# Two pairs of heads in one chain of the recurrence of a decoder layer

## The chip, the cores and the metric

The kernel runs on one core of a Trainium2 chip. The metric is the time of one execution on the device, in microseconds. A core has five engines that run side by side, each with its own list of instructions in a fixed order: PE (TensorE, matrix products), ACT (ScalarE), DVE (VectorE), POOL (GpSimd) and SP (SyncE, here the queue of weight loads). PE writes into PSUM, eight banks of 128 rows by 512 f32 values; ACT and DVE read it from there into SBUF, the on-chip memory in which operands of products lie.

## The reference

The layer is: a SwiGLU feed-forward, a mixer (windowed attention beside an RWKV-7 recurrence of 16 heads of size 64, both gated), cross-attention into a fixed memory, a second feed-forward, and a norm. There are 256 tokens and a model width of 2048, all in f32. The part that the change touches is the recurrence:

```python
def step(S, inp):
    r_t, w_t, k_t, v_t, a_t, b_t = inp
    sa = jnp.einsum('bhij,bhj->bhi', S, a_t)
    S = S * w_t[:, :, None, :] + sa[..., None] * b_t[:, :, None, :] + v_t[..., None] * k_t[:, :, None, :]
    return S, jnp.einsum('bhij,bhj->bhi', S, r_t)
```

The result y of each head is then normed over its 64 values, gets a bonus term and a gate, and goes through w_proj_rwkv.

## The kernel before, in words

Nearly all of PE's time goes into the dense products: weights come from HBM in units of two 128-row blocks by 512 columns, ACT rounds each unit to a high part (line 339), DVE forms the low part (line 340), and PE multiplies high by high, low by high and high by low (lines 412 to 414), 512 columns a product. All other work of the mixer is cut into small steps by Python generators, which `Interleave` keeps in groups. `product` calls `bg.tick()` after every six wide products, and a tick takes the next step of the first generators of each group, as many as the group's limit. So the order of instructions on each engine comes from when the steps are called, and a scheduler may then move an instruction behind others of its engine while what it needs isn't free.

The recurrence is computed without a loop over tokens, in two chunks of 128 tokens. Heads are treated in pairs, two heads of size 64 making 128 rows. There are 16 heads in two halves of eight (h = 0, 1); a half has four pairs j. A generator `pair(h, j)` (lines 1162 to 1252) carries one pair through both chunks c. In each chunk it does, a step a tick:

- the masked products (lines 1178 to 1189): three kinds (keys by removal, keys by receptance, removal keys by receptance), for each of the two heads e one product of 64 rows (rows 0 to 63 or 64 to 127), 128 x 128 results. Head e's three results go to a tr bank of its own, 384 of 512 columns; DVE multiplies each bank by the masks into mk, 128 x 384;
- u and nt (lines 1193 to 1206) into one tr bank, and two copies by ACT;
- v0, v1, w and sa (`stage`, lines 1210 to 1226), each two products of 64 columns into an mm bank and a copy of 128 x 128 by ACT, each needing the one before; in the first chunk also the transposes bk of the keys (lines 1228 to 1232) in a tr bank;
- the output y (lines 1236 to 1245): products whose result has 64 rows (L1238, L1240), for both heads, and in the first chunk the state s0 for the second (lines 1242 to 1250).

The generators stand in the group chain with limit 3: up to three pairs go on at the same time, and between two ticks stand six wide products. PSUM is shared: three banks acc (dense products), three mm, two tr. Everything else that needs a tr bank (transposes at line 600, norms, values) shares those two. SBUF tiles of 128 x 1024 come from a ring t4 of N4 = 20 slots. `finish` (from line 1257) norms y of two pairs, and the projection by w_proj_rwkv starts behind it.

Of the kernel before, what the change touches and what calls it, by code (L numbers as in the profile page):

```python
# [7 lines left out]
F32 = mybir.dt.float32  # L8
F32R = mybir.dt.float32r
AF = mybir.ActivationFunctionType  # L10
ALU = mybir.AluOpType
# [4 lines left out]
P = 128  # L16
T = 256
# [12 lines left out]

UP, DOWN = 2.0**40, 2.0**-40
GROUPS = ((0, 4), (4, 4), (8, 3))
N4 = 20

AHEAD, LOADED = 2, 4

# [96 lines left out]
def decoder_layer(ctx: ExitStack, tc: tile.TileContext, a: dict, out: bass.AP):  # L133
    nc = tc.nc
    act, dve, pool, pe = nc.scalar, nc.vector, nc.gpsimd, nc.tensor
# [32 lines left out]
    def idle(n):  # L168
        for _ in range(n):
            yield  # L170
# [596 lines left out]
    with tc.tile_pool(name="mx", bufs=1, reuse_waits="tile") as sp:  # L767
# [3 lines left out]
        def t4(name, shape=(P, 4, T), dt=F32):  # L771
            return sp.tile(list(shape), dt, tag="t4", name=name, bufs=N4)

# [378 lines left out]
                    pool.dma_start(r[q, :, : 32 * i], ld[q, o, : 32 * i])  # L1152
            xb[h, c] = x, r

        def small(name):
            return sp.tile([P, P], F32, tag="sm", name=name, bufs=14)

        rows = [slice(64 * e, 64 * e + 64) for e in range(2)]
        ek = dict(skip_group_check=True)
        yq = {}  # L1160

        def pair(h, j):
            yield from wait_for("inverse")
            yield from wait_for(f"ready{h}")
            if j % 2 == 0:
                yq[h, j // 2] = sp.tile([P, 2, T], F32, tag="yq", name="yq", bufs=3)
            y = yq[h, j // 2]
            if j == 0:
                for c in range(2):
                    inverse_blocks(h, c)  # L1170
            if j < 3:
                yield from idle(3 + j)
            ah, bh, kh, rh = at_[h], bt[h], aa[h], rt[h]
            s0 = None
            for c in range(2):
                cs_ = slice(c * P, (c + 1) * P)
                mk = sp.tile([P, 2, 3, P], F32, tag="mk", name="mk", bufs=3)
                b = [tr() for _ in range(2)]
                for m, (x1, x2) in enumerate(((kh, ah), (kh, rh), (bh, rh))):
                    for e, r in enumerate(rows):  # L1180
                        pe.matmul(  # L1181
                            b[e][:, m * P : (m + 1) * P], x1[r, j, cs_], x2[r, j, cs_],
                            start=True, stop=True,
                        )
                for e in range(2):
                    dve.tensor_tensor(
                        mk[:, e].rearrange("p m t -> p (m t)"), b[e][:, : 3 * P],
                        mask3[:].rearrange("p m t -> p (m t)"), ALU.mult,
                    )
                yield  # L1190
                vp = vtok[h][:, c, j * P : (j + 1) * P]
                x, rr = xb[h, c]
                b = tr()
                for e, r in enumerate(rows):
                    pe.matmul(b[:, r], mk[:, e, 0, :], vp[:, r], start=e == 0, stop=c == 0, **ek)
                if c:
                    pe.matmul(b[:, :P], ah[:, j, cs_], s0[:], start=False, stop=True, **ek)
                for e in range(2):
                    pe.matmul(
                        b[:, (2 + e) * P : (3 + e) * P], rr[:, 4 * e + j, :], x[:, 4 * e + j, :],  # L1200
                        start=False, stop=True, **ek,
                    )
                u = small("u")
                act.copy(u[:], b[:, :P])
                nt = sp.tile([P, 2, P], F32, tag="nt", name="nt", bufs=3)
                act.copy(nt[:], b[:, 2 * P :].rearrange("p (e t) -> p e t", e=2))
                yield
                vb = mm()

                def stage(lhs, rhs, o, first, name):  # L1210
                    for e, r in enumerate(rows):
                        pe.matmul(  # L1212
                            vb[:, o : o + P][:, r], lhs(e), rhs[:, r],
                            start=first and e == 0, stop=True, **ek,
                        )
                    s = small(name)
                    act.copy(s[:], vb[:, o : o + P])
                    return s

                v0 = stage(lambda e: x[:, 4 * e + j, :], u, 0, True, "v0")  # L1220
                yield
                v1 = stage(lambda e: nt[:, e, :], v0, 0, False, "v1")
                yield
                w = stage(lambda e: nt[:, e, :], v1, P, False, "w")
                yield
                sa = stage(lambda e: nt[:, e, :], w, 0, False, "sa")
                if c == 0:
                    b = tr()
                    pe.transpose(b[:, :P], bh[:, j, cs_], ident[:])
                    pe.transpose(b[:, P : 2 * P], kh[:, j, cs_], ident[:])  # L1230
                    bk = sp.tile([P, 2, P], F32, tag="bk", name="bk", bufs=3)
                    act.copy(bk[:], b[:, : 2 * P].rearrange("p (x f) -> p x f", x=2))
                yield
                b = tr()
                if c:
                    pe.matmul(b[:, :P], s0[:], rh[:, j, cs_], start=True, stop=False, **ek)
                for e, r in enumerate(rows):
                    pe.matmul(b[r, :P], vp[:, r], mk[:, e, 1, :], start=c == 0, stop=False, **ek)  # L1238
                for e, r in enumerate(rows):
                    pe.matmul(b[r, :P], sa[:, r], mk[:, e, 2, :], start=False, stop=True, **ek)  # L1240
                if c == 0:
                    bs = b[:, P : 2 * P]
                    pe.matmul(bs, bk[:, 0, :], sa[:], start=True, stop=False, **ek)
                    pe.matmul(bs, bk[:, 1, :], vp, start=False, stop=True, **ek)
                act.copy(y[:, j % 2, cs_], b[:, :P])
                if c == 0:
                    s0 = small("s0")
                    dve.scalar_tensor_tensor(
                        s0[:], bs, dec[h][:, j : j + 1], bdup, ALU.mult, ALU.mult
                    )  # L1250
                yield
            bg.seen.add(f"y{4 * h + j}")


        yr = Act([], [], 4)
# [257 lines left out]
```

## Time and profile before

| | us |
|---|---|
| median of 3 runs (2262.24 to 2262.78) | 2262.58 |
| the profiled execution | 2263.34 |
| its span, first to last instruction | 2261.6 |
| PE busy | 2246.8 |
| DVE busy | 1778.4 |
| ACT busy | 1226.9 |
| POOL busy | 132.2 |

The span is what lies between the first and the last instruction of the profiled execution; 1.7 us of its time lie outside. Busy time of an engine counts each moment once. A matrix product's length in the trace is its way through the array, and the next one starts before it ends: how long a product holds PE is read from start to start. A product in plain f32 (those of the small steps) shows as two records; a product of lines 412 to 414, whose operands are rounded, and a transpose show as one. A form such as 64*128 gives rows and columns of the array that a product uses.

### The profile page before, as it was taken

To read this page: it belongs to the slowest core of one execution; us is meant where nothing else is said; L and a number is where in the kernel's file an instruction comes from. 1 tells how busy PE (TensorE), PEld (TensorE's weight loads), DVE (VectorE), ACT (ScalarE), POOL (GpSimd) and SP (SyncE) were. 2 spreads that over 40 slices of the span, in tenths; PEclk is the share of its full clock that TensorE was granted. 3 is DMA by queue.
4 is the path that set the end of the run, shared out by engine and by line. 5 is a ranking of instruction groups with operands and counts; after the bars stand their busy time and mean duration, and the time that the engine had idled before them with its cause. 6 is when DMAs were issued, how large, how long until landed. Compare 5 with 4: busy or idle time off the path is not lost.

```text
span 2261.6 us, 28110 instructions
## 1 busy us (share of the span) xinstructions
PE 2246.8 (99%) x10617; PEld 1845.5 (82%) x10617; DVE 1778.4 (79%) x2281; ACT 1226.9 (54%) x1653; POOL 132.2 (6%) x192
## 2 busy tenths in 40 slices
PE   9999999999999999999999999999999999999998
PEld 7888888888888877788888888888888888888886
DVE  7899989998988477886434566547899988998987
ACT  6555555555556477444435446456555455555554
POOL 1000000000001000301220030001000000000002
PEclk9999999999999999999999999999999999999999
DMA  7555565555556544666433476647555565555564
GB/s 262 186 206 199 190 210 199 186 204 205 189 200 200 161 135 155 216 214 208 147 90 100 143 257 218 203 166 271 187 203 201 191 211 198 186 205 205 186 209 145
DMA packets 219144, 432.49 MB, mean 191 GB/s; under 512 B 14108, under 2 KB 16385, under 8 KB 219009
## 3 DMA queue, kind: packets, MB, share of 16 engines
q1 hardware_dynamic: 210432, 404.78, 52.7%
q0 software_dynamic: 8112, 25.12, 3.5%
q8 instruction: 83, 1.36, 0.2%
q10 hardware_dynamic: 464, 0.79, 0.1%
q14 instruction: 53, 0.43, 0.1%
HBM read 417.56 MB, written 13.11 MB: 190 GB/s over the span
## 4 chain that ended last, share of the span: by engine, by line
PE 96%; DVE 2%; issue 1%; DMA 1%; ACT 1%; SPq 0%; POOL 0%; POOLq 0%; DVEq 0%; ACTq 0%
PE acc L412 19%; PE acc L413 19%; PE acc L414 19%; PE mm L414 8%; PE mm L412 8%; PE mm L413 8%; PE tr L600 2%; PE tr L413 2%; PE tr L412 2%; PE tr L414 2%; PE mm L1212 1%; PE tr L1181 1%; DVE lo L340 1%; DMA raw<-in_w_out_dram 0%; PE mm L827 0%
## 5 line engine op out<-in xcount | busy, mean ns | idle before, releaser
L340 DVE TENSOR_TENSOR lo<-raw,hi 128x1024 fp32r<-128x1024 f32 (+1 forms) x770 | 894.0, 1163 | 352.9 <-ACT hi L339 351.2
L339 ACT CAST hi<-raw 128x1024 fp32r<-128x1024 f32 (+1 forms) x770 | 759.7, 997 | 747.5 <-PE acc L414 528.5
L412 PE MATMUL acc<-hi,xhi 128*128 128x512 f32 (+1 forms) x1196 | 477.7, 400 | 2.1 <-ACT xhi L627 1.7
L413 PE MATMUL acc<-lo,xhi 128*128 128x512 f32 (+1 forms) x1196 | 465.7, 389 | 0.0
L414 PE MATMUL acc<-hi,xlo 128*128 128x512 f32 (+1 forms) x1196 | 465.0, 389 | 0.0
L412 PEld LDWEIGHTS acc<-hi,xhi 128*128 128x128 f32 x1196 | 225.3, 188 | 52.1 <-issue 5.5
L413 PEld LDWEIGHTS acc<-lo,xhi 128*128 128x128 f32 x1196 | 225.2, 188 | 45.8 <-issue 3.2
L414 PEld LDWEIGHTS acc<-hi,xlo 128*128 128x128 f32 x1196 | 224.6, 188 | 46.5 <-DVE xlo L628 1.0
L347 ACT CAST thi<-raw 128x1024 fp32r<-128x1024 f32 x172 | 178.9, 1050 | 57.6 <-DVE raw L368 44.2
L348 DVE TENSOR_TENSOR tlo<-raw,thi 128x1024 fp32r<-128x1024 f32 x172 | 208.3, 1220 | 0.7 <-ACT thi L347 0.4
L412 PE MATMUL mm<-hi,xhi 128*128 128x512 f32 x380 | 149.5, 393 | 0.0
L414 PE MATMUL mm<-hi,xlo 128*128 128x512 f32 x380 | 148.3, 390 | 0.0
L413 PE MATMUL mm<-lo,xhi 128*128 128x512 f32 x380 | 148.3, 390 | 0.0
L413 PE MATMUL acc<-lo,hhi 128*128 128x512 f32 x372 | 145.7, 392 | 0.8 <-DVE lo L340 0.8
L414 PE MATMUL acc<-hi,hlo 128*128 128x512 f32 x372 | 145.7, 392 | 0.0
L412 PE MATMUL acc<-hi,hhi 128*128 128x512 f32 x372 | 145.1, 390 | 0.0
L414 PEld LDWEIGHTS mm<-hi,xlo 128*128 128x128 f32 x380 | 71.4, 188 | 15.0
L413 PEld LDWEIGHTS mm<-lo,xhi 128*128 128x128 f32 x380 | 71.4, 188 | 14.4
L412 PEld LDWEIGHTS mm<-hi,xhi 128*128 128x128 f32 x380 | 71.5, 188 | 14.4
L413 PEld LDWEIGHTS acc<-lo,hhi 128*128 128x128 f32 x372 | 69.9, 188 | 15.4 <-DVE lo L340 1.2
L412 PEld LDWEIGHTS acc<-hi,hhi 128*128 128x128 f32 x372 | 69.9, 188 | 14.3
L414 PEld LDWEIGHTS acc<-hi,hlo 128*128 128x128 f32 x372 | 70.0, 188 | 13.9
(384 smaller groups left out, 3550.2 us busy)
## 6 DMA issues: line engine op xcount, KB each, us to landing
raw<-in_ffn_w_up_dram SPq DMA_DIRECT2D x88, 1024.0 KB, 5.3
raw<-in_ffn_w_down_dram SPq DMA_DIRECT2D x88, 1024.0 KB, 5.1
raw<-in_ffn_w_gate_dram SPq DMA_DIRECT2D x84, 1024.0 KB, 5.1
raw<-in_w_in_dram SPq DMA_DIRECT2D x136, 512.0 KB, 3.5
raw<-in_w_out_dram SPq DMA_DIRECT2D x32, 512.0 KB, 4.4
raw<-in_w_proj_attn_dram SPq DMA_DIRECT2D x16, 512.0 KB, 3.8
raw<-in_w_proj_rwkv_dram SPq DMA_DIRECT2D x16, 512.0 KB, 5.9
raw<-in_w_cross_kv_dram SPq DMA_DIRECT2D x16, 512.0 KB, 3.7
```

Of the source, the lines that this page charges most:

```text
L339: at["hi"] = act.copy(hi[:, s], raw[:, s])
L340: at["lo"] = dve.tensor_tensor(lo[:, s], raw[:, s], f32(hi[:, s]), ALU.subtract)
L347: act.copy(hi[:], v[:])
L348: dve.tensor_tensor(lo[:], v[:], f32(hi[:]), ALU.subtract)
L412: pe.matmul(o, xh, hi, start=first, stop=False, **how)
L413: pe.matmul(o, xh, lo, start=False, stop=False, **how)
L414: pe.matmul(o, xl, hi, start=False, stop=last, **how)
L600: pe.transpose(b[:, o : o + P], tok[:, t, col : col + P], ident[:])
L1181: pe.matmul(b[e][:, m * P : (m + 1) * P], x1[r, j, cs_], x2[r, j, cs_], start=True, stop=True,)
L1212: pe.matmul(vb[:, o : o + P][:, r], lhs(e), rhs[:, r], start=first and e == 0, stop=True, **ek,)
```

## The change

One generator now carries two pairs. `pairs(h, q)` replaces `pair(h, j)`, with j = 2q and 2q + 1; the group chain has limit 2 in place of 3.

- The masked products come from a function `masked`, in three groups of eight for both chunks together, where there were two groups of six a pair: the first two kinds of chunk 0, the third kind of both chunks, and, after sa of chunk 0, the first two kinds of chunk 1. A head's bank is filled to 512 columns, and DVE's product with the masks is 128 x 512, into a tile of the ring t4.
- u, v0, v1, w, sa hold both pairs, 128 x 256, and ACT copies both at once; nt fills a tr bank of its own for both pairs, 128 x 512, while before it shared one with u.
- The transposes bk of both pairs are made in the v0 step and in an mm bank, before in the sa step and in a tr bank.
- The outputs of both pairs stand in one tr bank, and one copy by ACT writes both.
- N4 is 22 in place of 20. The tiles of mk no longer have a ring of their own; the other rings of the chain have fewer, larger slots.
- A generator idles 4 ticks (q = 0) or 8 (q = 1) before its first step, where pairs idled 3, 4, 5 and 0.

```diff
@@ -30,7 +30,7 @@
 UP, DOWN = 2.0**40, 2.0**-40
 GROUPS = ((0, 4), (4, 4), (8, 3))
-N4 = 20
+N4 = 22
 AHEAD, LOADED = 2, 4
@@ -145,7 +145,7 @@
     bg.group("feat", 1)
     bg.group("attn", 2)
     bg.group("ew", 1)
-    bg.group("chain", 3)
+    bg.group("chain", 2)
     bg.group("norm", 1)
     bg.group("mem", 1)
@@ -1152,104 +1152,153 @@
                     pool.dma_start(r[q, :, : 32 * i], ld[q, o, : 32 * i])
             xb[h, c] = x, r
-        def small(name):
-            return sp.tile([P, P], F32, tag="sm", name=name, bufs=14)
...
         rows = [slice(64 * e, 64 * e + 64) for e in range(2)]
         ek = dict(skip_group_check=True)
         yq = {}
-        def pair(h, j):
+        def small(name, tag="sm", bufs=6):
+            return sp.tile([P, 2, P], F32, tag=tag, name=name, bufs=bufs)
+        def masked(h, js, which):
+            sides = ((aa[h], at_[h]), (aa[h], rt[h]), (bt[h], rt[h]))
+            b = [tr() for _ in range(2)]
+            for i, (m, c) in enumerate(which):
+                cs_ = slice(c * P, (c + 1) * P)
+                x1, x2 = sides[m]
+                for k, j in enumerate(js):
+                    o = (2 * i + k) * P
+                    for e, r in enumerate(rows):
+                        pe.matmul(
+                            b[e][:, o : o + P], x1[r, j, cs_], x2[r, j, cs_], start=True, stop=True
+                        )
+            t = t4("mk", (P, 2, 4, P))
+            mask = mask3[:, :2] if which[0][0] == 0 else mask3[:, 1:]
+            for e in range(2):
+                dve.tensor_tensor(
+                    t[:, e].rearrange("p (m k) t -> p m k t", m=2),
+                    b[e][:].rearrange("p (m k t) -> p m k t", m=2, k=2),
+                    mask.unsqueeze(2).to_broadcast([P, 2, 2, P]), ALU.mult,
+                )
+            return t
+        def pairs(h, q):
             yield from wait_for("inverse")
             yield from wait_for(f"ready{h}")
...
+            js = (2 * q, 2 * q + 1)
+            y = yq[h, q] = sp.tile([P, 2, T], F32, tag="yq", name="yq", bufs=3)
+            if q == 0:
                 for c in range(2):
                     inverse_blocks(h, c)
...
+            yield from idle(4 + 4 * q)
             ah, bh, kh, rh = at_[h], bt[h], aa[h], rt[h]
...
+            s0 = later = None
             for c in range(2):
                 cs_ = slice(c * P, (c + 1) * P)
...
+                if c == 0:
+                    mk = masked(h, js, ((0, 0), (1, 0)))
+                    yield
+                    later = masked(h, js, ((2, 0), (2, 1)))
+                    yield
+                vp = [vtok[h][:, c, j * P : (j + 1) * P] for j in js]
+                x, rr = xb[h, c]
+                b = tr()
+                for k, j in enumerate(js):
                     for e, r in enumerate(rows):
                         pe.matmul(
...
+                            b[:, k * P : (k + 1) * P][:, r], mk[:, e, k, :], vp[k][:, r],
+                            start=k + e == 0, stop=c == 0, **ek,
                         )
...
+                    if c:
+                        pe.matmul(
+                            b[:, k * P : (k + 1) * P], ah[:, j, cs_], s0[:, k, :], start=False,
+                            stop=True, **ek,
+                        )
+                u = small("u")
+                act.copy(u[:], b[:, : 2 * P].rearrange("p (k f) -> p k f", k=2))
                 b = tr()
...
+                for k, j in enumerate(js):
+                    for e in range(2):
+                        o = (2 * k + e) * P
+                        pe.matmul(
+                            b[:, o : o + P], rr[:, 4 * e + j, :], x[:, 4 * e + j, :],
+                            start=o == 0, stop=True, **ek,
+                        )
+                nt = sp.tile([P, 4, P], F32, tag="nt", name="nt", bufs=2)
+                act.copy(nt[:], b[:].rearrange("p (k t) -> p k t", k=4))
+                yield
+                vb = mm()
+                def stage(lhs, rhs, o, first, name):
+                    for k in range(2):
+                        for e, r in enumerate(rows):
+                            pe.matmul(
+                                vb[:, (o + k) * P : (o + k + 1) * P][:, r], lhs(k, e), rhs[:, k, r],
+                                start=first and k + e == 0, stop=True, **ek,
+                            )
+                    s = small(name)
+                    act.copy(
+                        s[:], vb[:, o * P : (o + 2) * P].rearrange("p (k f) -> p k f", k=2)
+                    )
+                    return s
+                v0 = stage(lambda k, e: x[:, 4 * e + js[k], :], u, 0, True, "v0")
+                if c == 0:
+                    b = mm()
+                    for k, j in enumerate(js):
+                        for i, z in enumerate((bh, kh)):
+                            o = (2 * k + i) * P
+                            pe.transpose(b[:, o : o + P], z[:, j, cs_], ident[:])
+                    bk = sp.tile([P, 4, P], F32, tag="bk", name="bk", bufs=2)
+                    act.copy(bk[:], b[:].rearrange("p (x f) -> p x f", x=4))
+                yield
+                v1 = stage(lambda k, e: nt[:, 2 * k + e, :], v0, 0, False, "v1")
+                yield
+                w = stage(lambda k, e: nt[:, 2 * k + e, :], v1, 2, False, "w")
+                yield
+                sa = stage(lambda k, e: nt[:, 2 * k + e, :], w, 0, False, "sa")
+                yield
+                if c == 0:
+                    mk_next = masked(h, js, ((0, 1), (1, 1)))
+                    yield
+                b = tr()
                 if c:
...
+                    for k, j in enumerate(js):
+                        pe.matmul(
+                            b[:, k * P : (k + 1) * P], s0[:, k, :], rh[:, j, cs_], start=k == 0,
+                            stop=False, **ek,
+                        )
+                for k in range(2):
+                    o = slice(k * P, (k + 1) * P)
                     for e, r in enumerate(rows):
                         pe.matmul(
...
+                            b[r, o], vp[k][:, r], mk[:, e, 2 + k, :], start=c + k == 0, stop=False,
+                            **ek,
                         )
...
+                    for e, r in enumerate(rows):
+                        pe.matmul(
+                            b[r, o], sa[:, k, r], later[:, e, 2 * c + k, :], start=False, stop=True,
+                            **ek,
+                        )
                 if c == 0:
...
+                    for k in range(2):
+                        bs = b[:, (2 + k) * P : (3 + k) * P]
+                        pe.matmul(bs, bk[:, 2 * k, :], sa[:, k, :], start=False, stop=False, **ek)
+                        pe.matmul(bs, bk[:, 2 * k + 1, :], vp[k], start=False, stop=True, **ek)
+                act.copy(y[:, :, cs_], b[:, : 2 * P].rearrange("p (k t) -> p k t", k=2))
                 if c == 0:
...
+                    s0 = small("s0", "s0", 2)
+                    for k, j in enumerate(js):
+                        dve.scalar_tensor_tensor(
+                            s0[:, k, :], b[:, (2 + k) * P : (3 + k) * P], dec[h][:, j : j + 1],
+                            bdup, ALU.mult, ALU.mult,
+                        )
+                    mk = mk_next
+                yield
+            for j in js:
+                bg.seen.add(f"y{4 * h + j}")
         yr = Act([], [], 4)
@@ -1302,8 +1351,8 @@
             bv.append(t4("bv"))
             columns4(bv[h], 16 + 4 * h, f"v{h}")
             bg.spawn("ew", values(h))
-            for j in range(4):
-                bg.spawn("chain", pair(h, j))
+            for q in range(2):
+                bg.spawn("chain", pairs(h, q))
             for i in range(2):
                 bg.spawn("norm", finish(h, i))
```

More of the change, by code (lines that the diff above doesn't have):

```diff
@@ L1190, in pair @@
-                yield
-                vp = vtok[h][:, c, j * P : (j + 1) * P]
-                x, rr = xb[h, c]
-                b = tr()
[L1194 to L1202, printed above, removed]
@@ L1211, in stage @@
+                for k in range(2):
+                    o = slice(k * P, (k + 1) * P)
                     for e, r in enumerate(rows):
                         pe.matmul(
-                            vb[:, o : o + P][:, r], lhs(e), rhs[:, r],
-                            start=first and e == 0, stop=True, **ek,
-                        )
[L1216 to L1220, printed above, removed]
@@ L1233, in pair @@
[L1233 to L1244, printed above, removed]
```

43 lines of the change are left out of this document (3 added, 40 removed).

## The prediction

> **What bounds the kernel now.** I read the page's first parts, then the waits, then the stretch in which the changed code runs, then the order of PE's instructions there, row by row.
>
> ```profile
> span 2261.6 us, 28110 instructions
> PE 2246.8 (99%) x10617; PEld 1845.5 (82%) x10617; DVE 1778.4 (79%) x2281; ACT 1226.9 (54%) x1653; POOL 132.2 (6%) x192
> PEclk9999999999999999999999999999999999999999
> PE 96%; DVE 2%; issue 1%; DMA 1%; ACT 1%; SPq 0%; POOL 0%; POOLq 0%; DVEq 0%; ACTq 0%
> ```
>
> PE is busy for 99% of the span and is 96% of the chain that ended last, at a full clock. The kernel ends when PE has issued its instructions. The changed chain runs from about 1104 us to 1285 us (L1181, its first products, starts at 1106.8). The view by windows for that stretch, and PE's own waits in it:
>
> ```profile
> core 0: us, PE busy (x) PEld busy (x) DVE busy (x) ACT busy (x) POOL busy (x), PEclk, DMA share, GB/s
> 1104.00:1285.00 181.00, 180.59 (x1185) 151.08 (x1184) 77.56 (x97) 79.08 (x177) 25.29 (x42) 1.00 0.33 99
> PE tr L1195 <- DVE mk L1186: 0.4, 2, 0.2
> ```
>
> PE idles 0.4 us of 181; DVE and ACT are busy for 43% and 44%, DMA for a third. So fewer ACT and DVE instructions buy nothing by themselves, and a gain can only come from PE's rows lying closer together. PE's number of matrix products does not change: the built order has 10,060 in both kernels. What changes is which stand next to each other, and the timeline shows that this has a price.
>
> **A masked group whose products alternate between the two heads of a pair (rows 0 to 63, rows 64 to 127), and one whose products don't.** Start, length, engine, line; each f32 product is two records. The timeline of PE:
>
> ```profile
> 1106.46 0.39 PE L414 MATMUL acc<-hi,xlo 128*128 128x512 f32 x1
> 1106.78 0.49 PE L1181 MATMUL tr<-at,aa 64*128 64x128 f32 x4
> 1107.10 0.39 PE L1181 MATMUL tr<-rt,aa 64*128 64x128 f32 x4
> 1107.33 0.39 PE L1181 MATMUL tr<-rt,kk 64*128 64x128 f32 x4
> 1107.65 0.50 PE L412 MATMUL acc<-hi,xhi 128*128 128x512 f32 x1
> ...
> 1111.27 0.49 PE L1181 MATMUL tr<-at,aa 64*128 64x128 f32 x2
> ...
> 1112.83 0.51 PE L412 MATMUL acc<-hi,xhi 128*128 128x512 f32 x1
> ...
> 1115.93 0.50 PE L412 MATMUL acc<-hi,xhi 128*128 128x512 f32 x1
> 1116.36 0.49 PE L1181 MATMUL tr<-at,aa 64*128 64x128 f32 x2
> ...
> 1117.23 0.50 PE L413 MATMUL acc<-lo,xhi 128*128 128x512 f32 x1
> ```
>
> The first group (six products, heads in turn) holds PE for 1107.65 - 1106.78 = 0.87 us: two heads run side by side, twelve records in six slots of 0.11 us (1107.33 - 1107.10 for two slots), plus about 0.1 us going in and as much going out. The second (three of one head, then three of the other) takes 1112.83 - 1111.27 = 1.56 us: every record has a slot of its own. Half a group alone (the third) takes 0.87 us, as long as a whole alternating one. The built order decides this: where the second head's bank is not yet free, its products are placed behind.
>
> ```profile
> L1181 PE MATMUL tr<-at,aa x64: 271/323/374, 1106.8 to 1257.9; 64*128 64x128 f32 x64
> ```
>
> There are 16 such groups (64 records of the first form, four a group). The chain of waits merges those that stand in one piece (start, length, what):
>
> ```profile
> 1111.34 1.56 PE tr L1181 x12
> ...
> 1138.22 1.62 PE tr L1181 x12
> 1145.12 1.62 PE tr L1181 x12
> ...
> 1166.71 1.30 PE tr L1181 x11
> ...
> 1187.49 1.28 PE tr L1181 x11
> 1189.14 1.26 PE tr L1181 x11
> ```
>
> By the built order, 3 groups alternate (0.87 each, 2.6 us); 3 alternate in part (1.30 above, and two of 0.87 in the timeline, 3.0); 5 stand as three and three (the other rows above, 7.3); 5 are cut in halves with other work between (10 x 0.86 = 8.6). Sum 21.6 us.
>
> **After: 12 groups of eight products.** Eight of them alternate fully: 0.87 + 2 x 0.11 = 1.09 each, 8.7 us. One is 2, 2, then alternating: 1.3. Two stand as four and four: the 1.26 to 1.62 of three and three plus 4 x 0.11, so 1.70 to 2.06; I take 1.75, since the cheaper rows have the same waits ahead (a freed bank, none inside the half): 3.5. One is cut in halves: 2 x (0.86 + 0.22) = 2.2. Sum 15.7, a gain of **5.9 us**. Bounds: all twelve alternating 13.1 (gain 8.5), none 12 x 2.06 = 24.7 (loss 3.1).
>
> **The output products** (L1238, L1240; 64 columns, two heads side by side already) and going into such a group:
>
> ```profile
> 1127.26 0.39 PE L413 MATMUL acc<-lo,xhi 128*128 128x512 f32 x1
> 1127.48 0.40 PE L414 MATMUL acc<-hi,xlo 128*128 128x512 f32 x1
> 1127.81 0.44 PE L1238 MATMUL tr<-mk,vtok 128*64 128x128 f32 x4
> 1128.08 0.39 PE L1240 MATMUL tr<-mk,sa 128*64 128x128 f32 x4
> 1128.40 0.49 PE L1243 MATMUL tr<-sa,bk 128*128 128x128 f32 x2
> ```
>
> Four products take 1128.40 - 1127.81 = 0.59 us, 16 times, 9.4 us. Eight in one go take 0.59 + 4 x 0.11 = 1.03, 8 times, 8.2: **1.2 us** less (nothing, if each pair paid its own switch; 1.4 at 1.0 each). Going in costs 0.33 (1127.48 to 1127.81) where one product follows another in 0.22 to 0.23: 0.1 us. Before, PE goes in 21 + 16 = 37 times, after 13 + 8 = 21: 16 x 0.095 = **1.5 us** less.
>
> **Work with one answer.** Full products of the chain (L1195, L1199, L1212 and the others) keep their count and their 0.11 us a record, grouped or not: 0. Transposes of the keys move from the sa step into the v0 step and from the two tr banks to the mm ring: same count, 0 (if mm's three banks ran out, a wait of the size below). ACT loses 60 copies, DVE 8 products:
>
> ```profile
> L1217 ACT COPY v<-mm 128x128 f32<-128x128 f32 x32 | 8.4, 267 | 6.1 <-PE mm L1212 5.9
> L1206 ACT COPY nt<-tr 128x256 f32<-128x256 f32 x16 | 6.1, 379 | 0.0
> L1186 DVE TENSOR_TENSOR mk<-tr,mask 128x384 f32<-128x384 f32 x32 | 16.9, 553 | 15.1 <-PE tr L1181 15.0
> L1136 DVE TENSOR_TENSOR bv<-tr,bv 128x512 f32<-128x512 f32 x3 | 2.1, 692 | 7.3 <-PE tr L1131 7.3
> L340 DVE TENSOR_TENSOR lo<-raw,hi 128x1024 fp32r<-128x1024 f32 x30 | 36.6, 1218 | 64.5 <-ACT hi L339 64.5
> xb<-xd POOLq DMA_DIRECT2D x16, 32.0 KB, 3.5
> ```
>
> A copy of double width takes 0.38 in place of 2 x 0.27; all of it lies beside PE, 0. Masks now take slots of the t4 ring and wait there for older loads of xb and rb; by the order, what POOL itself waits for before it issues the ones for the second half of the heads ends some 250 products ahead of their first use, against 3.5 us of landing: 0. If that cover were gone, one landing, 3.5 us, would be on PE's path. SP issues the same 522 instructions in the same order: 0. The last output group stands 30 places earlier than before, so the norm and projection behind it wait no longer.
>
> **Waits.** Two stalls show before, and both are of a product behind a mask:
>
> ```profile
> 1109.14 0.39 PE L412 MATMUL acc<-hi,xhi 128*128 128x512 f32 x1
> 1109.71 0.43 PE L1195 MATMUL tr<-vtok,mk 128*128 128x64 f32 x2 [0.18 <-DVE mk L1186]
> ...
> 1260.02 0.39 PE L412 MATMUL acc<-hi,xhi 128*128 128x512 f32 x1
> 1260.63 0.66 PE L1195 MATMUL tr<-vtok,mk 128*128 128x64 f32 x4 [0.23 <-DVE mk L1186]
> ```
>
> 0.57 and 0.61 us where 0.23 is usual: 0.7 us together. They may go. New ones: a mask product now covers 128x512 from PSUM, nearest row L1136, 0.69. A masked group follows another 5 times, both tr banks full, with at least one block of six wide products between, 6 x 0.227 = 1.36 us, against a record's tail of 0.27 and two masks, 1.38, together 1.65: up to 0.3 us each if DVE is free. At one place v1 follows v0 with four transposes (0.44) between, against 0.27 + 0.38: 0.2. I take 1.2 us in all, net **+0.5**; bounds -0.7 (none) and +3.0 (half of the twelve groups meet 0.6 us, half an L340).
>
> On these waits the Trainium skill speaks against the change: "TensorEngine Tiling", section Performance Considerations, says that tiling speeds up the products but not the emptying of PSUM, which may then become the bottleneck. By that rule the time would be that of the first rival below, 2272; by the rows, with both emptying engines at 44%, it is the sum.
>
> **Sum.** -5.9 - 1.2 - 1.5 + 0.5 = -8.1 us. The profiled execution took 2263.34 us (0.76 above the median 2262.58): it would become 2255.2, the median **2254.5**. Its own range, with stalls from -0.7 to +3 and the groups of four and four at either price, is 2251.5 to 2257.5.
>
> **Rivals.** *The two tr banks become the bound* (slower). Each masked group now fills both banks; if DVE has an L340 in front each time, the second bank is free after 0.27 + 1.22 + 1.38 = 2.87 us, 1.5 us beyond the 1.36 of cover; 12 x 1.5 = 18 us, so 2254.5 + 18 = 2272. It decides from 1.1 us a group. For it: DVE takes its queue in order, and the two stalls above are this. Against: of 16 groups before, two showed it, and L340 comes only 30 times in 181 us. 0.04. *Half of it*: 6 groups x 1.0 = 6, 2260.5, no change to be measured. 0.04.
>
> *The heads don't run side by side in groups of eight*: the order alternates them, and the chip would still give a slot to each record. Then masked groups cost 24.7, a loss of 3.1 against gains of 1.2 + 1.5 and the 0.5: 2262.9. For it: only three full groups show alternation; against: all three take 0.87. 0.05.
>
> *More than forecast*: all small waits inside the groups (the 1.56 to 1.62 against 1.28) go: 2250.5. 0.05.
>
> **How the numbers follow.** The forecast has 0.82. About 0.2%, 4.5 us, is what a measurement of this kernel can tell from no change: faster is below 2258.1. Faster 0.82 + 0.05 = 0.87; same 0.04 + 0.05 = 0.09; slower 0.04. The range 2251.5 to 2259.0 leaves out the rivals and a little of the forecast's tail.
>
> **What would show it.** In the profile after: PE about 99% busy in a span near 2253; masked groups with starts of equal form in x4 or x8 rows and 1.1 us from first to next line, about 15.7 us over all; eight output groups of 1.0 us; PE waits on mk below 2 us. The forecast is wrong if those groups last 2 us, if rows of the products behind them begin with idle time ended by DVE, or if PE's records outside the chain are later than before, by less than the chain gained.

## The result, and the profile after

The changed kernel takes 2254.95 us (median of 7 runs, 2254.39 to 2255.57); the kernel before, on the same chip, 2262.46 (7 runs, 2262.24 to 2262.79). The ratio is 0.9967, 95% interval 0.9958 to 0.9976: faster by 0.33%, 7.5 us. The page of the profile after:

```profile
span 2253.2 us, 28023 instructions
PE 2237.3 (99%) x10617; PEld 1838.2 (82%) x10617; DVE 1775.7 (79%) x2273; ACT 1223.1 (54%) x1593; POOL 134.0 (6%) x192
PEclk9999999999999999999999999999999999999999
```

PE is still busy for 99% of the span at a full clock, with as many records as before (10,617), and the span is 8.4 us shorter. The same stretch of PE's order, some 760 products from just ahead of the chain to its end (1176 records in either view), in the view by windows, first before and then after (columns as in the prediction):

```profile
1103.82:1282.76 178.94, 178.53 (x1176) 149.36 (x1175) 75.35 (x95) 78.39 (x177) 23.32 (x39) 1.00 0.32 97
```

```profile
1103.43:1273.76 170.33, 168.96 (x1176) 143.62 (x1175) 77.26 (x93) 72.73 (x115) 23.17 (x39) 1.00 0.35 97
```

178.94 us became 170.33, 8.6 less: the whole gain lies where the chain runs. PE now idles 1.4 us there, where it idled 0.4. The timeline of PE after, at the chain's first groups (L1173 is the old L1181, L1210 the old L1195):

```profile
1107.44 0.39 PE L414 MATMUL acc<-hi,xlo 128*128 128x512 f32 x1
1107.76 0.71 PE L1173 MATMUL tr<-at,aa 64*128 64x128 f32 x8
1108.31 0.61 PE L1173 MATMUL tr<-rt,aa 64*128 64x128 f32 x8
1108.85 0.50 PE L412 MATMUL acc<-hi,xhi 128*128 128x512 f32 x1
1109.19 0.39 PE L413 MATMUL acc<-lo,xhi 128*128 128x512 f32 x1
1109.42 0.40 PE L414 MATMUL acc<-hi,xlo 128*128 128x512 f32 x1
...
1112.57 0.39 PE L413 MATMUL acc<-lo,xhi 128*128 128x512 f32 x1
1112.80 0.40 PE L414 MATMUL acc<-hi,xlo 128*128 128x512 f32 x1
1113.51 0.66 PE L1210 MATMUL tr<-vtok,mk 128*128 128x64 f32 x4 [0.32 <-DVE mk L1179]
```

A masked group of eight, heads in turn, holds PE for 1108.85 - 1107.76 = 1.09 us, as forecast. The last row is a new stall: 0.71 us from start to start, where 0.23 is usual. The waits of PE name it and its like (L600 stands behind the stretch, and is taken up at the end):

```profile
PE tr L1276 <- DVE mk L1179: 0.7, 2, 0.4
PE tr L600 <- DVE x L1403: 0.6, 2, 0.3
PE tr L1322 <- ACT gr L1364: 0.3, 1, 0.3
PE tr L1210 <- DVE mk L1179: 0.3, 1, 0.3
```

Two output products (L1276, 0.43 and 0.38 us more than usual from start to start), finish's first product (L1322, 0.51), u (L1210, 0.48) and one v1 behind v0 (0.18) add 1.98 us. Every one but v1 is a product that asks for a tr bank.

Splitting the stretch by what holds PE (from the start of a record to the next start):

| us | before | after | difference | forecast |
|---|---|---|---|---|
| masked groups | 21.6 | 15.5 | -6.1 | -5.9 |
| output products | 9.4 | 8.2 | -1.2 | -1.2 |
| other products, without stalls | 147.2 | 144.7 | -2.5 | -1.5 |
| stalls outside masked groups | 0.7 | 2.0 | +1.3 | +0.5 |
| the stretch | 178.9 | 170.3 | -8.6 | -8.1 |

### The profile page after: what moved, and what is told of

It reads as the page before. It is cut to its first block, busy times and chain, and to the rows that moved or that the text cites. A ratio compares the mean times of both kernels' runs of the same rounds, so it can differ in the third digit from the quotient of the medians.

```text
span 2253.2 us, 28023 instructions
## 1 busy us (share of the span) xinstructions
PE 2237.3 (99%) x10617; PEld 1838.2 (82%) x10617; DVE 1775.7 (79%) x2273; ACT 1223.1 (54%) x1593; POOL 134.0 (6%) x192
## 4 chain that ended last, share of the span: by engine, by line
PE 47%; DVE 2%; DMA 1%; issue 0%; ACT 0%; POOLq 0%; POOL 0%; DVEq 0%; ACTq 0%
PE acc L412 9%; PE acc L414 9%; PE acc L413 9%; PE mm L414 4%; PE mm L413 4%; PE mm L412 4%; PE mm L1237 1%; PE tr L600 1%; PE tr L413 1%; PE tr L414 1%; PE tr L412 1%; DVE lo L340 1%; PE tr L1173 0%; DMA raw<-in_w_out_dram 0%; PE tr L1225 0%
## 5 line engine op out<-in xcount | busy, mean ns | idle before, releaser
L340 DVE TENSOR_TENSOR lo<-raw,hi 128x1024 fp32r<-128x1024 f32 (+1 forms) x770 | 894.2, 1163 | 345.6 <-ACT hi L339 343.9
```

Of the source, the lines that this page charges most:

```text
L340: at["lo"] = dve.tensor_tensor(lo[:, s], raw[:, s], f32(hi[:, s]), ALU.subtract)
```

## The experiments

The theory to be tested: the gain is heads side by side (row halves of the array in turn), fewer entries into small tiles, and one stretch of PE; ACT and DVE lie beside. Rivals: it is the wider, fewer instructions behind PE; the two tr banks are close to being the bound; alternation alone would do it. "Against before" is the difference to the median of the kernel before that ran beside it on the same chip.

| kernel | us | ratio to before, 95% interval | against before |
|---|---|---|---|
| the change | 2254.95 | 0.9967 [0.9958, 0.9976] | -7.5 |
| e1, change, heads apart | 2257.90 | 0.9980 [0.9972, 0.9989] | -4.2 |
| e2, change, outputs apart | 2257.58 | 0.9980 [0.9971, 0.9989] | -4.6 |
| e3, change, copies apart | 2254.47 | 0.9966 [0.9954, 0.9978] | -7.7 |
| e4, before, other ring | 2256.76 | 0.9976 [0.9967, 0.9985] | -5.4 |
| e5, change, other ring | 2251.65 | 0.9953 [0.9940, 0.9965] | -10.7 |
| e6, e5, finish too, other idling | 2251.93 | 0.9954 [0.9942, 0.9967] | -10.4 |
| e7, change, masks twice | 2256.40 | 0.9974 [0.9964, 0.9984] | -6.0 |
| e8, before, heads apart | 2263.47 | 1.0005 [0.9996, 1.0014] | +1.1 |
| e9, e5 and u | 2251.48 | 0.9952 [0.9940, 0.9965] | -10.9 |
| e10, e9 and finish | 2250.80 | 0.9950 [0.9938, 0.9963] | -11.5 |
| e11, e10, other idling | 2250.52 | 0.9948 [0.9935, 0.9962] | -11.8 |

### e1: the heads of a group apart

```diff
-            for i, (m, c) in enumerate(which):
-                cs_ = slice(c * P, (c + 1) * P)
-                x1, x2 = sides[m]
-                for k, j in enumerate(js):
-                    o = (2 * i + k) * P
-                    for e, r in enumerate(rows):
+            for e, r in enumerate(rows):
+                for i, (m, c) in enumerate(which):
+                    cs_ = slice(c * P, (c + 1) * P)
+                    x1, x2 = sides[m]
+                    for k, j in enumerate(js):
+                        o = (2 * i + k) * P
                         pe.matmul(
...
```

> The changed kernel; in a masked group the four products of one head stand before the four of the other. Products, banks, copies and their places stay; only the order inside the group changes, so the two heads can't run side by side. Theory (the gain is mainly the two heads side by side): the ten groups that alternate, 1.09 us each, become like the three that stood apart (1.64, 1.83, 2.17 us), so ten times 0.55 to 0.75: 2260.5 to 2262.5 us. Rival (the gain is fewer, wider instructions and fewer handovers, and alternation is worth nothing): 2255.0.

2257.90 us, 3.3 us less gain than the change (3.0 in the stretch): neither. The nine groups that had their heads in turn (nine, not ten) each took 0.55 us more, the theory's lower price: ten groups of 1.64, one of 1.83 and one in halves of 1.09 add up to 20.4 us where the change has 15.5, 4.9 more. The first of them, in PE's timeline:

```profile
1107.83 0.71 PE L1173 MATMUL tr<-at,aa 64*128 64x128 f32 x4
1108.38 0.27 PE L1173 MATMUL tr<-rt,aa 64*128 64x128 f32 x1
1108.39 0.37 PE L1173 MATMUL tr<-at,aa 64*128 64x128 f32 x1
1108.49 0.27 PE L1173 MATMUL tr<-rt,aa 64*128 64x128 f32 x1
...
1108.93 0.61 PE L1173 MATMUL tr<-rt,aa 64*128 64x128 f32 x4
1109.47 0.50 PE L412 MATMUL acc<-hi,xhi 128*128 128x512 f32 x1
```

The second head's first product (at, 1108.39) starts although three records of the first head, which stand ahead of it in the order (rt, from 1108.49), are still to come. Sixteen slots of 0.11 us and 0.2 for the ways in and out would be 1.96; the group takes 1.64, three slots less. So heads one after the other in the order are still side by side for three of eight slots. The edit takes away five of them, 0.55 us, and not the whole overlap, as the expectation has it.

Besides, all four stalls on a tr bank are gone (stalls 0.18 us in place of 1.98). The timelines tell why. First the change, DVE and then PE, around the output at 1206.35 us:

```profile
1204.47 1.23 DVE L340 TENSOR_TENSOR lo<-raw,hi 128x1024 fp32r<-128x1024 f32 x1 [3.33 <-ACT hi L339]
1205.62 1.28 DVE L1179 TENSOR_TENSOR mk<-tr,mask 128x512 f32<-128x512 f32 x2
```

```profile
1206.35 0.44 PE L1276 MATMUL tr<-mk,vtok 128*64 128x128 f32 x4 [0.36 <-DVE mk L1179]
```

And e1, the same place:

```profile
1207.19 0.69 DVE L1179 TENSOR_TENSOR mk<-tr,mask 128x512 f32<-128x512 f32 x1 [3.30 <-PE tr L1173]
1207.80 1.22 DVE L340 TENSOR_TENSOR lo<-raw,hi 128x1024 fp32r<-128x1024 f32 x1
1208.93 0.68 DVE L1179 TENSOR_TENSOR mk<-tr,mask 128x512 f32<-128x512 f32 x1
```

```profile
1209.22 0.44 PE L1276 MATMUL tr<-mk,vtok 128*64 128x128 f32 x4
```

With heads in turn both banks are full at the same time, and both masks stand behind a split of weights (L340, 1.23 us); the first bank is free at 1206.3, and the output starts then. With heads apart the first bank is full half a microsecond earlier in the group, its mask goes ahead of the split, and the bank is free at 1207.9, well before the output at 1209.22. So heads in turn rather than one after the other save 4.9 us of PE in this kernel, and 1.8 of it is paid back as waits for a bank.

### e8: the same in the kernel before

```diff
-                for m, (x1, x2) in enumerate(((kh, ah), (kh, rh), (bh, rh))):
-                    for e, r in enumerate(rows):
+                for e, r in enumerate(rows):
+                    for m, (x1, x2) in enumerate(((kh, ah), (kh, rh), (bh, rh))):
```

> The kernel before, with the three products of one head ahead of the three of the other in all 16 masked groups, as was done to the changed kernel: what then differs between the two is the grouping alone. The three groups of 0.87 us and two of those in part become 1.28, 2.0 us more; the two waits behind a mask (0.7 together) may go, as they did there. Theory (grouping alone, with no head beside another, is worth some 5 us of the 7.5): 2263.5 within 0.7, that is 5.6 above the changed kernel with heads apart, 2257.9. Rival (alternation is all, grouping nothing): 2258.

2263.47 us, 1.1 above the kernel before (the interval of the ratio holds 1) and 5.6 above e1: the theory's number. With e1 this splits the 7.5 us. Grouping, with the heads one after the other on both sides: from +1.1 to -4.2 against before, 5.3 us. Heads in turn are worth 3.3 us net after the change and were worth 1.1 before it, so 2.2 us more. In the stretch the first part is larger: 180.0 us in e8, 173.3 in e1, 6.7 less (masked groups 23.2 to 20.4, outputs 9.4 to 8.2, the products around them 147.4 to 144.7), which leaves 1.9 of the stretch's 8.6 to heads in turn. Most of the rest of the difference lies behind the stretch, where e1 takes 1.0 us longer than e8 (172.2 against 171.2 over 800 records).

The split isn't clean. Five groups of e8 take 1.19 us where twelve slots and 0.2 would be 1.52, so there too the heads overlap for three slots. An estimate from 0.11 a slot and 0.2 a piece: of the 2.8 us that the masked groups lose from e8 to e1, eight pieces fewer are 1.6, and most of the rest is that more groups overlap in this way.

### e4: the kernel before with its tr banks relieved

```diff
                 x, rr = xb[h, c]
-                b = tr()
+                b = mm()
...
-                    b = tr()
+                    b = mm()
                     pe.transpose(b[:, :P], bh[:, j, cs_], ident[:])
...
-                b = tr()
+                b = mm()
                 if c:
                     pe.matmul(b[:, :P], s0[:], rh[:, j, cs_], start=True, stop=False, **ek)
```

> The kernel before, still one pair a chain and three chains, but the first products of a step (u and nt), the transposes and the outputs take banks of the mm ring, so that masked products alone use the two tr banks with the rest of the kernel. By the built order 10 of the 16 masked groups then alternate in place of 3. Theory (alternation is the gain, and the change gets it by fewer claims on two banks): masked groups 21.6 us become 17.1, 4.5 less: 2258.0 within 0.7. Rival (the grouping itself, fewer entries and wider instructions, is what pays): 2262.5, no change.

2256.76 us: 5.4 us faster than before by three words, 0.9 more than expected. Masked groups add up to 17.0 us (expected 17.1); besides, the stalls outside them fell from 0.7 to 0.3 us. The timeline of a group that before stood three and three at 1.62 us:

```profile
1137.27 0.49 PE L1181 MATMUL tr<-at,aa 64*128 64x128 f32 x4
1137.60 0.39 PE L1181 MATMUL tr<-rt,aa 64*128 64x128 f32 x4
1137.82 0.39 PE L1181 MATMUL tr<-rt,kk 64*128 64x128 f32 x4
1138.14 0.44 PE L1238 MATMUL mm<-mk,vtok 128*64 128x128 f32 x4
```

It takes 0.87 us, and the output behind it, now in an mm bank, starts at once. The rival (only grouping pays) falls: with no grouping at all, relieved banks and the alternation that they allow are worth about as much as the grouping with heads apart.

### e2: the outputs of the two pairs apart

```diff
-                if c:
-                    for k, j in enumerate(js):
+                for k, j in enumerate(js):
+                    if c:
                         pe.matmul(
...
-                for k in range(2):
                     o = slice(k * P, (k + 1) * P)
                     for e, r in enumerate(rows):
...
-                if c == 0:
-                    for k in range(2):
+                    if c == 0:
                         bs = b[:, (2 + k) * P : (3 + k) * P]
```

> The changed kernel; full products (of the state) stand between the output products of the first and of the second pair, so PE goes into the 64-column form 16 times in place of 8, with the same products. Theory (each entry costs 0.1 us and the way out as much): 8 x 0.16 to 0.25, 1.3 to 2.0 us more, 2256.3 to 2257.0. Rival (a change of form costs nothing; the 0.1 us before was something else): 2255.0 within 0.3.

2257.58 us, 2.9 less gain than the change: more than the theory's 1.3 to 2.0. In the stretch it is 2.8 us (173.15 against 170.33) for eight more trips into the 64-column form, 0.35 a trip. The timeline of PE in e2 has one:

```profile
1207.82 0.44 PE L1275 MATMUL tr<-mk,vtok 128*64 128x128 f32 x4 [0.36 <-DVE mk L1179]
1208.09 0.39 PE L1280 MATMUL tr<-mk,sa 128*64 128x128 f32 x4
1208.41 0.49 PE L1286 MATMUL tr<-sa,bk 128*128 128x128 f32 x2
1208.73 0.39 PE L1287 MATMUL tr<-vtok,bk 128*128 128x128 f32 x2
1209.05 0.44 PE L1275 MATMUL tr<-mk,vtok 128*64 128x128 f32 x4
1209.32 0.39 PE L1280 MATMUL tr<-mk,sa 128*64 128x128 f32 x4
```

Two records take 0.22 us as a rule. The way out (1208.09 to 1208.41), the first full product after it (1208.41 to 1208.73) and the way in (1208.73 to 1209.05) take 0.32 each: 0.1 us at three places, and 0.05 on the first output product (1209.05 to 1209.32, 0.27). The way between row-tiled and wide products is alike in the profile after: 1109.19 - 1108.85 = 0.34 for the first wide product behind a group, 0.23 for the next. Elsewhere the first full product behind a trip has 64 columns and loses 0.05, not 0.1 (0.16 in place of 0.11 for its first record), so a trip costs 0.3 to 0.35 us. The Trainium skill says in a general form what this looks like ("TensorEngine Tiling (Array Packing)", section Tiling Modes, under Key Properties: changing the mode, not just the tile, drains the TensorEngine) and gives no price. The rows here fit that, though they show the loss of time and not the drain.

### e3: ACT's copies apart

```diff
-                u = small("u")
-                act.copy(u[:], b[:, : 2 * P].rearrange("p (k f) -> p k f", k=2))
+                u = small("u")
+                for k in range(2):
+                    act.copy(u[:, k, :], b[:, k * P : (k + 1) * P])
...
```

> The changed kernel with its ACT copies of the chain split back, one for each pair: 60 more ACT instructions of 0.27 us where one took 0.38. Matrix products and their order stay. Theory (ACT lies beside PE): 2255.0 within 0.5. Rival (the chain's handovers are on the path, so a longer copy delays the next stage): 40 handovers x 0.15 us, 6 us more, 2261.

2254.47 us, as fast as the change (7.7 and 7.5 against before). The copies of `stage` for v0 and v1, by the groups of instructions, in the change and in e3:

```profile
L1242 ACT COPY v<-mm 128x256 f32<-128x256 f32 x16 | 5.9, 371 | 14.3 <-PE mm L1237 14.2
```

```profile
L1245 ACT COPY v<-mm 128x128 f32<-128x128 f32 x32 | 7.0, 268 | 14.0 <-PE mm L1239 13.8
```

The wider copies are cheaper for ACT and worth nothing to the time.

### e7: every mask twice

```diff
-            for e in range(2):
+            for e in (0, 0, 1, 1):
                 dve.tensor_tensor(
                     t[:, e].rearrange("p (m k) t -> p m k t", m=2),
```

> The changed kernel with every mask product on DVE made twice, into the same place: 24 more of 0.69 us, 16.6 us more of DVE's work, and every tr bank of a masked group held 0.7 or 1.4 us longer. By the built order two more groups lose part of their alternation and one is cut: 1.3 us more. Theory (the masks lie beside PE but for four or five places): 1.3 us and 0.7 to 1.4 us at each of four places: 2259 to 2262. Rival (the two tr banks are nearly the bound of the stretch): nearly all of the 16.6 us, 2268 to 2271. Second rival (masks are hidden): 2256.

2256.40 us, 1.5 less gain than the change: the theory's 2259 to 2262 is out, and so is the first rival; the time is near the second. DVE's groups, the change and e7:

```profile
L1179 DVE TENSOR_TENSOR mk<-tr,mask 128x512 f32<-128x512 f32 x24 | 15.5, 682 | 4.0 <-PE tr L1173 3.7
```

```profile
L1179 DVE TENSOR_TENSOR mk<-tr,mask 128x512 f32<-128x512 f32 x48 | 30.4, 683 | 9.7 <-PE tr L1173 9.2
```

14.9 us more of DVE, and PE's stretch grows by 1.1 us (171.38 against 170.33). Masked groups take 1.3 us more (16.8 against 15.5), since the alternation of a few more breaks; the stalls don't grow (2.0 to 1.3 us), since the order puts more wide products ahead of what waits (nine in place of six ahead of the first u). So the two tr banks are no bound. Here the emptying of PSUM costs by breaking the order of the heads, and by single waits. The Trainium skill's warning ("TensorEngine Tiling (Array Packing)", section Performance Considerations, under PSUM Bottleneck: tiling doesn't make the emptying of PSUM faster, and after a fourfold speedup of the products it may become the bottleneck) isn't borne out as a bound in this kernel, where two heads at most are side by side.

### e5, e9, e10, e11: which bank the waiting products want

e5 is the change with nt and the outputs in mm banks; e9 adds u; e10 adds finish's two products; e11 starts the second pair at 4 + 5q. e6 is e11 without u's part.

```diff
+++ e5
-                b = tr()
+                b = mm()
                 for k, j in enumerate(js):
                     for e in range(2):
                         o = (2 * k + e) * P
...
-                b = tr()
+                b = mm()
                 if c:
                     for k, j in enumerate(js):
+++ e9, besides
-                b = tr()
+                b = mm()
                 for k, j in enumerate(js):
                     for e, r in enumerate(rows):
+++ e10, besides
-            b = tr()
+            b = mm()
             pe.matmul(b[:], bdmean[:], sq[:], start=True, stop=True)
...
-            b = tr()
+            b = mm()
             for k in range(2):
                 o = b[:, k * T : (k + 1) * T]
+++ e11, besides
-            yield from idle(4 + 4 * q)
+            yield from idle(4 + 5 * q)
```

> The changed kernel with the products nt and the outputs in banks of the mm ring, in place of the two tr banks; nothing else. By the built order 11 of the 12 masked groups then alternate: the one of 1.83 us and the one in halves (2.17) become 1.09 each, 1.8 us less. Theory (what is left of the cost is claims on the two tr banks): besides, the two waits of an output product on a bank that a mask still reads (0.43 and 0.38 us) go: 2.6 us less, 2252.2, and up to 0.5 more at each of two places if a mask then stands behind a split of weights on DVE: 2252.2 to 2253.2. Rival (the waits are for the masks themselves and stay, and what the groups save is waited for): 2254.9, no change against the changed kernel.

2251.65 us, 3.2 us better than the change, past the theory's 2252.2; the rival is out. Masked groups add 13.7 us (1.8 less, as expected). DVE, and then PE, where the change waited at 1206.35:

```profile
1204.27 1.23 DVE L340 TENSOR_TENSOR lo<-raw,hi 128x1024 fp32r<-128x1024 f32 x1 [3.33 <-ACT hi L339]
1205.41 1.28 DVE L1179 TENSOR_TENSOR mk<-tr,mask 128x512 f32<-128x512 f32 x2
```

```profile
1205.39 0.40 PE L414 MATMUL acc<-hi,xlo 128*128 128x512 f32 x1
1205.72 0.44 PE L1276 MATMUL mm<-mk,vtok 128*64 128x128 f32 x4
```

The masks come at the same point of the work, behind the same split, and the output starts while they run: it never needed them, only a bank.

> As e5_ring (nt and outputs in the mm ring), and the product u, the first to read a mask, takes its bank from the mm ring too. The built order of PE is the same as in e5_ring. Theory (the 0.48 us that u stands idle at 1113.5 us is not for its mask, which was ready, but for a tr bank that the next group's mask still reads): that wait goes, 2251.65 - 0.5 = 2251.2. Rival (it waits for the mask itself): 2251.65, no change.

2251.48 us. The time can't be told from e5 (5 runs each, 2251.13 to 2251.97 against 2251.37 to 2251.93); the trace can. PE and DVE at u:

```profile
1113.00 0.39 PE L414 MATMUL acc<-hi,xlo 128*128 128x512 f32 x1
1113.23 1.00 PE L1210 MATMUL mm<-vtok,mk 128*128 128x64 f32 x8
```

```profile
1112.98 1.28 DVE L1179 TENSOR_TENSOR mk<-tr,mask 128x512 f32<-128x512 f32 x2
```

u follows in 0.23 us, while the masks that held its bank in the change are still being made: that wait was for the bank as well, and the stretch is 0.6 us shorter than in e5 (166.65 against 167.27). What hides it in the two profiled executions is another wait, behind the chain, of transposes on the sum with x1d's blocks, which differs from profile to profile. In the waits of e5 and e9:

```profile
PE tr L600 <- DVE x L1403: 0.3, 1, 0.3
```

```profile
PE tr L600 <- DVE x L1403: 1.1, 2, 0.9
```

PE's order is not quite the same in the two, other than the expectation says: in one group u stands ahead of nt in e9 and behind it in e5. But the change has 0.6 us there and e3, whose order differs from it in the place of one wide product, 1.2, so the wait varies with hardly a change of order too.

> As e9_ring_u, and the two products of finish take mm banks. By the built order one masked group then stands as two and six in place of four and four (1.5 us in place of 1.64). Theory (the 0.51 us ahead of finish's first product is for a tr bank too): 0.6 us below e9_ring_u, 2250.6. Rival (the wait is for the input of finish, or the mm ring is now the short one): 2251.2 or above.

2250.80 us. finish's wait of 0.51 us went. The masked group behind it is cut in two and six, which costs 0.1 us more in the group and another trip, and its first piece starts 0.69 us after the last record of finish, where 0.53 is usual. So the stretch is only 0.1 us shorter than in e9 (166.53 against 166.65); the 0.7 us between the medians can't be put down to this edit, and the intervals overlap.

> As e10_ring_u_finish, with the second pair starting at 4 + 5q idle steps, so that by the built order all 12 masked groups alternate: 13.1 us. Theory: 0.4 us below e10_ring_u_finish, and no wait of u in this order either (0.48 and 0.29 in e6_all_alternate): 2250.3 to 2251.0. Rival (this order has waits of its own on masks, as e6_all_alternate did): 2251.5.

2250.52 us, the lowest median, 4.4 us below the change (4.3 by the differences to before). All twelve groups alternate in the order; one waits inside and takes 1.60 us, the others 1.09, 13.6 in all where 13.1 was expected. Without u's part the same order gave:

> As the one before, and the two products of the norm behind the chain (finish) in the mm ring too, and the second pair starting at 4 + 5q idle steps in place of 4 + 4q. By the built order all 12 masked groups alternate: 13.1 us in place of 15.5. Theory: 2.4 us less, and the waits on a tr bank (0.43, 0.38 and 0.51 us) go: 3.7 us less, 2251.2, or 2252.2 if masks behind DVE's splits give 1 us back. Rival (alternation beyond nine groups is given back as waits for masks): 2254.9.

2251.93 us, no better than e5: this order has its own stalls (0.48 and 0.29 at u, and a masked group of 1.59 us), of which u's two are gone in e11. So of the change's claims on the two tr banks some 4 us could still be had, most of it by e5's two words.

## Why the prediction was right, and where it wasn't

The median came out at 2254.95, 0.45 above the forecast 2254.5, and the stretch lost 8.6 us where the sum said 8.1. The profiled execution of before lay 0.9 above the median of these 7 runs, that of after on its own, so the medians differ by 7.5. By the prediction's own steps:

- **What bounds.** Right: PE's time in the stretch decides. e3 (60 more copies) and e7 (14.9 us more of DVE) change it by nothing and by 1.1 us.
- **Masked groups, -5.9.** Measured -6.1. A group of eight with heads in turn took 1.09, as worked out; the one of 2, 2 and then in turn 1.10, not 1.3; the two of four and four 1.64 and 1.83, not 1.75 each; the one in halves 2.17. Two readings behind these numbers were off. Three and three doesn't give every record a slot of its own: that holds for the 1.56 and 1.62, where the second head starts behind the last record of the first; in the rows of 1.26 and 1.28 it starts before, and e1 shows four and four at 1.64 by the same overlap. It is also why two and two at the start can cost nothing (1.10, and 0.88 in two groups of before). And heads in turn are only a part of the step: e1 and e8 show that with the heads one after the other on both sides the masked groups would still have lost 2.8 us, from 23.2 to 20.4.
- **Output products, -1.2.** Measured -1.2.
- **Entries, -1.5.** Too small: the products around lost 2.5 us. The step priced the way in alone, 0.095 us, 16 times. e2 shows that a trip costs three such gaps and a half. Those inside the tiled group are in the two terms above; but the first full product behind it also loses 0.05 to 0.11 us, and that was in no term. Sixteen ways in and this make up the 2.5.
- **Waits, +0.5.** Too small, by 0.8 us: the old ones of 0.7 didn't leave 1.2 but 2.0 of new ones. The place was wrong too. The step looked for a masked group that waits for the one ahead; the scheduler moves those apart instead (four and four). What waits is what comes next and wants any bank of the same ring: u, the outputs, finish. e5 shows it for the outputs, e9 for u, e10 for finish. v1 behind v0 was foreseen (0.2) and measured (0.18).
- **Copies, masks, transposes, POOL, SP: 0.** For the copies e3 shows it. The transposes, POOL's loads and SP's issues were not tried alone; no wait on them stands in the chain's stretch.
- **Behind the chain: 0.** The 800 records after the stretch took 171.85 us before and 172.25 after. The difference is the wait of transposes (L600) on the sum with x1d's blocks: 0.3 us before, 0.6 after. One profile of each doesn't settle whether the change does that (e3, with nearly the change's order, has 1.2). But e4 and e8, with the old grouping, have none of this wait, and the ten profiles with the new one have 0.3 to 1.2, so some tenths of the gain are probably lost there. This was in no term, and its cause stays open.
- **Rivals.** *The two tr banks become the bound*: out by e7. *Half of it*: out as priced (6 us), though its mechanism, a bank behind a split of weights on DVE, is what the new stalls are, 1.8 us of them. *Heads don't run side by side in groups of eight*: out by the 1.09 us. *More than forecast*: its small waits, by its own measure 1.0 us in three groups (1.56 and twice 1.62 against 1.28), are down to 0.2 (1.83 against 1.64), but 1.3 came back outside the groups.
- **The range.** Its lower end doesn't follow from what it names: with all stalls gone and four and four at 1.70 the sum gives 2253.2, not 2251.5. The measured 2254.95 lies within either.

So the number was near for a reason that is partly luck: two terms missed by about a microsecond each, on opposite sides.

## What to carry to other kernels

When small products share an array that wide ones keep busy, count the changes of form, not the products: each trip into a tiled form cost 0.3 to 0.35 us here, three times what one way in shows. Products on different halves of the array run side by side when the order has them close: with heads in turn, or two and two at the start, a group of eight took 1.09 to 1.10 us, with four and four 1.64. Which order is built hangs on whether both their banks are free; relieving the ring of banks gave 5.4 us before the change and 3.2 to 4.3 after it, for a few words. When a group gets denser, look at what asks next for the ring that it fills, not only at who reads its result.

## What was not expected of the hardware

A full product behind a change of form is itself slower: 0.32 in place of 0.22 us, and 0.34 in place of 0.23 for a wide one, although its operands are ready. A product can start before others that stand ahead of it in PE's order: in e1 the second head's first record, on the other half of the array, starts at 1108.39, and three of the first head's come at 1108.49 and later. And heads side by side cost the waits of others: saving 4.9 us on PE was worth 3.0 in the stretch and 3.3 in the medians, because both banks of a group then fill at the same moment and both masks land behind the same 1.23 us on DVE.
